# Alternating load queues, a fourth buffer for `a`, a seventh for the output and an earlier load of `a` in a tuned batched 64x64 matmul

## The chip, the cores and the metric

The kernel runs on one core of a Trainium2 chip. The metric is the device time of a run in microseconds, given as the median of a kernel's runs. Times of single events are microseconds from the start of the profiled span.

## The reference

```python
def reference(a, b):                       # a, b: (1024, 64, 64) float32
    return np.matmul(a, b).astype(np.float32)
```

There are 1024 independent products of 64x64 matrices: 16.78 MB of a, 16.78 MB of b and 16.78 MB of output cross the pipe to memory, 50.33 MB in all.

## The kernel before

The work is cut into 16 b tiles of 64 matrices (one output tile each) and 8 a tiles of 128 matrices, so that each a tile serves two b tiles. VectorE regroups an a tile (`regroup`), TensorE transposes it, ScalarE copies the transposes out of PSUM, and VectorE spreads them into block-diagonal operands (`spread`). ScalarE casts the b tile to bf16, TensorE multiplies, and the two halves of an output tile are copied out of PSUM by ScalarE (first half) and VectorE (second half). Three queues carry the transfers: SyncE's and ScalarE's bring b and the first a tile, and GpSimd's brings all other a tiles (casting them from fp32 to bf16 on the way) and takes all stores. The parts that the change and the argument touch:

```python
    A_AHEAD = 3                            # a buffers
    B_AHEAD = 4                            # b buffers
    ...
    o_pool = ...tile_pool(name="o_pool", bufs=6)             # output tiles in SBUF
    o_psum = ...tile_pool(name="o_psum", bufs=2, space=PSUM) # two half tiles of products
    ...
    def load_a(s):                         # 4 DMAs on GpSimd's queue
        a_sb = a_pool.tile([128, 4, 16, 64], bf16, name="a_sb")
        for h in range(4):
            nc.gpsimd.dma_start(out=..., in_=a_v[s, h])
    ...
    def load_b(t):
        b_sb = b_pool.tile([128, 16, 128], fp32, name="b_sb")
        queue = nc.scalar if t in (1, 4, 6, 7) else nc.sync
        queue.dma_start(out=b_sb[:], in_=b_v[t])
    ...
        for half in range(2):              # in multiply(t)
            o_ps = o_psum.tile([128, 4, 2, 2, 64], fp32, name="o_ps")
            ...                            # 32 matmuls
            copy = nc.vector.tensor_copy if half else nc.scalar.copy
            evacuate(o_ps, 4 * half, 4, copy)
    ...
        load_first_a()
        ...
        for t in range(B_AHEAD):
            load_b(t)
        nc.vector.memset(bd_tiles[0][:], 0.0)
        make_identity(nc, identity)
        nc.gpsimd.memset(bd_tiles[1][:], 0.0)
        for s in range(1, A_AHEAD):
            load_a(s)
        regroup(0)
        transpose(0, 0)
        transpose(0, 1)
        spread(0)
        cast(0)
        regroup(1)
        load_a(A_AHEAD)
        transpose(1, 0)
        for t in range(n_t):
            s, half = t // 2, t % 2
            if t + 1 < n_t:
                spread(t + 1)
                cast(t + 1)
            if t + B_AHEAD < n_t:
                load_b(t + B_AHEAD)
            if half == 0:
                if s + 2 < n_s:
                    regroup(s + 2)
                if s + 1 + A_AHEAD < n_s:
                    load_a(s + 1 + A_AHEAD)
            multiply(t)
            ...
            if t >= HOLD - 1:
                store(t - HOLD + 1)        # on GpSimd's queue
```

"b3" below is the b tile with t = 3; "the second a tile" is the one with s = 1, "the seventh" the one with s = 6. In the page's line numbers, L99 is the regrouping, L121 the spread, L165 the copies of the products, L177 the products.

## Time and profile before

The median was 135.51 us. The profiled run was 0.3 us slower than that (135.82) and had this course.

| before | us |
|---|---|
| second a tile landed / its regrouping began | 27.92 / 28.04 |
| seventh a tile's regrouping began, after a wait of 2.56 | 96.58 |
| VectorE's last copy ended | 128.80 |
| last store landed | 132.55 |
| span / outside the span | 134.04 / 1.78 |

Read it as one line: VectorE starts a long run with the second a tile, works nearly without a pause, stops once for the seventh a tile, and 3.75 us after its last copy the last store lands. The prediction shows the profile's lines for it. Two more views are needed later. The first is the page's list of queues (queue, kind, packets, MB, share of the 16 DMA engines' time): q0 is GpSimd's, q1 SyncE's, q10 ScalarE's.

```profile
q0 software_dynamic: 8448, 24.12, 61.7%
q1 hardware_dynamic: 6624, 13.63, 28.7%
q10 hardware_dynamic: 2400, 5.24, 10.3%
q8 instruction: 9, 0.15, 0.4%
```

SyncE carries 12 b tiles and ScalarE 4. Queue 8 moved nine packets of 16 KB, which look like TensorE's own instructions: the kernel has 1,152 matmuls and 1,152 weight loads, and 2,304 is nine times 256 (e14 below, with 256 and 256, has two such packets). The second view is the list of queues between 20 and 27 us alone, while the second a tile is on its way:

```profile
q0 software_dynamic: 491, 0.91, 68.5%
q1 hardware_dynamic: 492, 0.97, 40.6%
```

Two queues are at work, and they get the same number of packets.

### The profile page before, as it was taken

The numbers are of one execution on the slowest core, as the hardware profiler recorded it, in microseconds if no ns is written. First come the engines' busy times: TensorE is split into PE (matmuls) and PEld (weight loads), VectorE is DVE, ScalarE is ACT, GpSimd is POOL, SyncE is SP. The second block draws the span as 40 slices with busy tenths as digits, with TensorE's granted clock in tenths as the row PEclk, the third lists the DMA queues.
The fourth block names the chain that finished last, engine by engine and source line by source line (L and its number), as shares of the span: only waits on it lengthen the run. The fifth ranks groups of instructions, "written<-read, shape, count | busy, mean of one in ns | idle before, by whom it ended". The sixth has DMA issues, their size and how long they took to land.

```text
span 134.0 us, 2820 instructions
## 1 busy us (share of the span) xinstructions
PE 66.2 (49%) x1152; PEld 61.9 (46%) x1152; DVE 105.5 (79%) x145; ACT 86.4 (64%) x125; POOL 43.7 (33%) x55
## 2 busy tenths in 40 slices
PE   0008206903970495849734863696309564466300
PEld 0008106904960485749624752685209463456300
DVE  5720539169899989998999999999299999999940
ACT  3244343991899287959998796679708999363500
POOL 8981215332313240214322244324004031141460
PEclk9999975797799768686998699559955999555555
DMA  3999999999999999999999999999999999999793
GB/s 67 386 360 305 306 284 273 267 301 305 302 280 289 281 396 332 310 289 350 402 359 279 269 367 399 351 270 275 390 397 395 393 397 398 402 406 362 262 313 112
DMA packets 17484, 43.17 MB, mean 322 GB/s; under 512 B 1088, under 2 KB 1088, under 8 KB 17472
## 3 DMA queue, kind: packets, MB, share of 16 engines
q0 software_dynamic: 8448, 24.12, 61.7%
q1 hardware_dynamic: 6624, 13.63, 28.7%
q10 hardware_dynamic: 2400, 5.24, 10.3%
q8 instruction: 9, 0.15, 0.4%
q14 instruction: 3, 0.02, 0.0%
HBM read 33.55 MB, written 16.78 MB: 375 GB/s over the span
## 4 chain that ended last, share of the span: by engine, by line
DMA 62%; DVE 14%; issue 11%; POOL 9%; POOLq 1%; DVEq 0%
DMA a_sb<-in_a_dram 45%; DMA out_dram<-o_sb 17%; DVE o_sb L165 8%; DVE at_bd L121 6%; POOL out_dram L154 3%; POOL a_sb L67 3%; POOL at_bd L205 3%; POOLq L262 1%; POOL identity masks.py:199 0%; DVE a_bf L99 0%; POOL identity masks.py:197 0%; POOLq L154 0%; DVEq L99 0%; POOLq masks.py:199 0%; DVEq L121 0%
## 5 line engine op out<-in xcount | busy, mean ns | idle before, releaser
L177 PEld LDWEIGHTS <-at_bd 128*128 128x128 bf16 x1024 | 43.8, 114 | 45.3 <-DVE o_sb L165 30.4
L177 PE MATMUL o_ps<-b_bf,at_bd 128*128 128x64 bf16 x960 | 43.1, 215 | 40.2 <-DVE o_sb L165 28.5
L121 DVE COPY at_bd<-at_sb 32x1024 f32<-32x1024 f32 x64 | 46.6, 728 | 7.3 <-ACT at_sb L111 5.3
L165 ACT COPY o_sb<-o_ps 64x512 f32<-64x512 f32 x60 | 34.8, 580 | 17.4 <-PE o_ps L177 10.7
L165 DVE COPY o_sb<-o_ps 64x512 f32<-64x512 f32 x60 | 41.3, 689 | 2.2 <-PE o_ps L177 1.3
L154 POOL DMA_DIRECT2D out_dram<-o_sb x20 | 20.9, 1044 | 46.6 <-DVE o_sb L165 22.8
L108 PE MATMUL at_ps<-identity,a_bf 128*128 128x128 f32 x128 | 22.8, 339 | 17.6 <-ACT a_bf L97 10.6
L67 POOL DMA_DIRECT2D a_sb<-in_a_dram x28 | 18.7, 681 | 38.9 <-DMA a_sb<-in_a_dram 28.1
L132 ACT CAST b_bf<-b_sb 128x2048 bf16<-128x2048 f32 x15 | 28.6, 1908 | 3.5 <-DMA b_sb<-in_b_dram 3.5
L108 PEld LDWEIGHTS at_ps<-identity,a_bf 128*128 128x128 f32 x128 | 19.1, 181 | 17.9 <-issue 10.6
L111 ACT COPY at_sb<-at_ps 128x512 f32<-128x512 f32 x32 | 17.8, 588 | 8.3 <-PE at_ps L108 8.1
L99 DVE COPY a_bf<-a_sb 128x4096 bf16<-128x4096 bf16 x7 | 8.6, 1227 | 9.0 <-DMA a_sb<-in_a_dram 8.8
L97 ACT CAST a_bf<-o_sb 128x1024 bf16<-128x1024 f32 x2 | 2.1, 1044 | 4.6 <-DMA o_sb<-in_a_dram 4.6
L165 ACT COPY o_sb<-at_ps 64x256 f32<-64x256 f32 x8 | 2.9, 367 | 3.1 <-PE at_ps L177 3.0
L177 PE MATMUL at_ps<-b_bf,at_bd 128*128 128x64 bf16 x64 | 3.6, 242 | 1.3 <-DVE at_bd L121 1.3
L203 DVE MEMSET at_bd<- 128x4096 f32 x1 | 3.5, 3472 | 0.8 <-issue 0.8
L97 DVE CAST a_bf<-o_sb 128x1024 bf16<-128x1024 f32 x2 | 1.5, 764 | 3.0 <-DMA o_sb<-in_a_dram 3.0
L205 POOL MEMSET at_bd<- 128x4096 f32 x1 | 3.5, 3509 | 0.0
L165 DVE COPY o_sb<-at_ps 64x256 f32<-64x256 f32 x8 | 3.4, 422 | 0.1
L200 ACT ACT_TABLE_LOAD x1 | 1.3, 1283 | 2.3 <-issue 2.3
L139 ACT CAST b_bf<-b_sb 128x512 bf16<-128x512 f32 x2 | 1.1, 614 | 0.4 <-DMA b_sb<-in_b_dram 0.4
L137 DVE CAST b_bf<-b_sb 128x512 bf16<-128x512 f32 x2 | 0.8, 426 | 0.0
(9 smaller groups left out, 1.5 us busy)
## 6 DMA issues: line engine op xcount, KB each, us to landing
out_dram<-o_sb POOLq DMA_DIRECT2D x14, 1024.0 KB, 22.5
a_sb<-in_a_dram POOLq DMA_DIRECT2D x28, 256.0 KB, 19.9
o_sb<-in_a_dram ACTq DMA_DIRECT2D x2, 512.0 KB, 6.9
o_sb<-in_a_dram SPq DMA_DIRECT2D x2, 512.0 KB, 5.9
out_dram<-o_sb POOLq DMA_DIRECT2D x2, 512.0 KB, 6.2
out_dram<-o_sb POOLq DMA_DIRECT2D x4, 256.0 KB, 3.9
b_sb<-in_b_dram SPq DMA_DIRECT2D x12, 0.5 KB, 20.2
b_sb<-in_b_dram ACTq DMA_DIRECT2D x4, 0.5 KB, 16.2
```

What stands on the lines that cost most here:

```text
L67: nc.gpsimd.dma_start(out=a_sb[:, h, :, :].rearrange("p v k -> p (v k)"), in_=a_v[s, h])
L97: copy(a_bf[:, :, h, :], a_sb[h].rearrange("p (v k) -> p v k", v=16))
L99: nc.vector.tensor_copy(a_bf[:], a_sb[:].rearrange("p h v k -> p v h k"))
L108: nc.tensor.transpose(at_ps[:, vo, :], a_cols[:, 4 * vo + 2 * j + wl, :], identity[:])
L111: nc.scalar.copy(at_tiles[s][:, j, :, wl, :, :], at_ps[:].rearrange("p vo (g mp) -> p g mp vo", mp=4),)
L121: nc.vector.tensor_copy(bd[rows, :, :, :, h, :].rearrange("p j g wl mo -> p j (g wl) mo"), at_tiles[t // 2][rows, :, half, :, :, :].rearrange(
L132: nc.scalar.copy(b_bf[:], b_sb[:])
L154: nc.gpsimd.dma_start(out=o_v[t, :, lo : lo + n, :], in_=o_sb[:, lo : lo + n].rearrange("p gh j wl n -> p (gh j wl n)"),)
L165: copy(dst, src)
L177: nc.tensor.matmul(o_ps[:, gl, g % 2, j, :], at_bd[:, j, g, :, u], b_bf[:, g, 64 * u : 64 * u + 64], start=(u == 0), stop=(u == 1),)
L203: nc.vector.memset(bd_tiles[0][:], 0.0)
L205: nc.gpsimd.memset(bd_tiles[1][:], 0.0)
```

## The change

The intent: share the b loads evenly between two queues, bring the second a tile earlier by issuing it after half of GpSimd's memset, and run further ahead with a. The whole diff:

```diff
-    A_AHEAD = 3
+    A_AHEAD = 4
@@
-    o_pool = ctx.enter_context(tc.tile_pool(name="o_pool", bufs=6))
+    o_pool = ctx.enter_context(tc.tile_pool(name="o_pool", bufs=7))
@@ def load_b(t):
-        queue = nc.scalar if t in (1, 4, 6, 7) else nc.sync
+        queue = nc.scalar if t % 2 else nc.sync
@@
-        for t in range(B_AHEAD):
+        for t in range(3):
             load_b(t)
         nc.vector.memset(bd_tiles[0][:], 0.0)
         make_identity(nc, identity)
-        nc.gpsimd.memset(bd_tiles[1][:], 0.0)
-        for s in range(1, A_AHEAD):
+        nc.gpsimd.memset(bd_tiles[1][:, 0], 0.0)
+        load_a(1)
+        nc.gpsimd.memset(bd_tiles[1][:, 1], 0.0)
+        for s in range(2, A_AHEAD):
             load_a(s)
         regroup(0)
         transpose(0, 0)
         transpose(0, 1)
+        load_b(3)
         spread(0)
```

Note the last line: b3 no longer starts with the other first tiles. It is issued by ScalarE, after ScalarE's share of the first transposes.

## The prediction

> **What bounds the kernel now.** I read the page's slices first (forty slices of 3.35 us; digits are tenths busy), to see which resource never rests.
>
> ```profile
> DVE  5720539169899989998999999999299999999940
> ...
> DMA  3999999999999999999999999999999999999793
> GB/s 67 386 360 305 306 284 273 267 301 305 302 280 289 281 396 332 310 289 350 402 359 279 269 367 399 351 270 275 390 397 395 393 397 398 402 406 362 262 313 112
> ...
> HBM read 33.55 MB, written 16.78 MB: 375 GB/s over the span
> ```
>
> The DMA row is 9 from the second slice to the thirty-seventh. The dips in GB/s are no slack: the row counts what is written, and the a tiles are read as fp32 and written as bf16. Summing the trace's packet records by what they read, every stretch of 5 us from 5 to 120 us moves 392 to 412 GB/s, whatever the mix, mean 397. The kernel moves 50.33 MB; at 397 GB/s that is 126.8 us of the 134.0 us span. By 5 us 0.73 MB have moved, 1.85 us' worth, so the start loses 3.15 us. After 120 us 3.82 MB are left, 9.6 us' worth, and they take until the last landing at 132.55: 2.95 us lost, in gaps where the queue waits for results. So if nothing in the transfers gets faster, scheduling can win 2.95 us at most: 135.5 - 2.95 = 132.55 us, 2.2% less.
>
> What decides those 2.95 us is VectorE, whose last copies release the last stores. Its timeline, in parts:
>
> ```profile
> 14.94 2.83 DVE L121 COPY at_bd<-at_sb 32x1024 f32<-32x1024 f32 x4 [5.33 <-ACT at_sb L111]
> ...
> 19.87 1.23 DVE L99 COPY a_bf<-a_sb 128x4096 bf16<-128x4096 bf16 x1 [2.10 <-DMA a_sb<-in_a_dram]
> ...
> 21.02 2.84 DVE L121 COPY at_bd<-at_sb 32x1024 f32<-32x1024 f32 x4
> ```
>
> ```profile
> 28.04 1.23 DVE L99 COPY a_bf<-a_sb 128x4096 bf16<-128x4096 bf16 x1 [4.18 <-DMA a_sb<-in_a_dram]
> ...
> 90.93 3.09 DVE L121 COPY at_bd<-at_sb 32x1024 f32<-32x1024 f32 x4
> 96.58 1.23 DVE L99 COPY a_bf<-a_sb 128x4096 bf16<-128x4096 bf16 x1 [2.56 <-DMA a_sb<-in_a_dram]
> ...
> 125.31 3.49 DVE L165 COPY o_sb<-at_ps 64x256 f32<-64x256 f32 x8
> ```
>
> L99 regroups an a tile (128 matrices, two b tiles). VectorE waits 4.18 us for the second a tile (landed 27.92), runs from 28.04 to 94.02 with pauses under half a microsecond (65.98 us for five a tiles, 13.2 each), waits 2.56 us for the seventh, then runs without a break to 128.8. The chain of waits says the same: the stations before the final run are these loads.
>
> ```profile
> 8.59 19.32 DMA a_sb<-in_a_dram
> ...
> 55.32 21.07 DMA a_sb<-in_a_dram
> ...
> 76.67 19.88 DMA a_sb<-in_a_dram
> ...
> 96.58 0.04 DVE a_bf L99
> ```
>
> So the time is: landing of the second a tile, plus VectorE's work, plus stalls on the way, plus some 5 us of last stores. ScalarE also waits twice for stores that still hold an output buffer (1.75 us before 84.5, 4.32 us before 100.56), beside VectorE's own wait.
>
> **What the Trainium skill says.** "DMA: Bandwidth & Descriptors", section "Issuing engines are not separate DMA queues": all transfers run on the same 16 engines, and several issuers save issue time only. The trace agrees: 403 GB/s with three queues loaded (10 to 15 us), 397 with two (20 to 25 us). The same page, "Queues, rings and completion order": an engine serves the queues in turn, a packet each. That agrees too, and decides the shares: b packets are 2 KB, a packets read 4 KB, and from 10 to 15 us SyncE, ScalarE and GpSimd move 108, 108 and 188 GB/s, near 1:1:2; from 20 to 25 us, with ScalarE's queue empty, 141 and 256. "SBUF — State Buffer", section "SBUF: two separate sides": a two-port VectorE operation locks GpSimd out of writing descriptors. Nothing before 4.7 us tests it here, but it could eat part of the early issue below, since VectorE's memset runs from 1.70 to 5.17.
>
> **Part 1, the split memset.** GpSimd's memset is 3.51 us, and its first a issue starts at 4.71. Half of it (1.75 us) after 1.25 puts the issue at 3.0. The first GpSimd packet followed the issue by 3.9 us (8.61); the same lag gives 6.9. The pipe is full from about 4.5 us, so these 1.7 us are taken from others: at a third of 397 GB/s 0.22 MB, which delays a tile 0 (landed 9.47) by some 0.7 us to 10.2. The first tile on GpSimd (2.10 MB) gets 0.43 MB by 10.2 at 132 GB/s; the other 1.66 MB at 190 take 8.7 us: landing 19.0 instead of 19.75. The second memset half ends near 7.3 and is needed only at about 20: free.
>
> **Part 2, b3 and the odd b tiles on ScalarE's queue.** Before, that queue is empty from 18.66 to 27.6 us, and GpSimd has two thirds of the pipe: its second tile lands at 27.92. After, b3 is issued near 14.4 us, behind b1, and fills just this stretch, so GpSimd stays near 190 GB/s: 2.10 MB / 0.190 = 11.0 us, landing at 19.0 + 11.0 = 30.0. b2 lands near 28.8, so it stays behind this. VectorE's regroup moves from 28.04 to 30.1: 2.1 us worse. Later odd tiles are issued on ScalarE after the cast of b(t+1), not at once after that of b(t), one step of 6.6 us later. Against that they no longer queue behind even tiles: at 108 GB/s a b tile (1.05 MB) takes 9.7 us, and with 3.7 us before the first packet about 13.4 of the 20 us available.
>
> **Part 3, four a buffers, seven output buffers.** In GpSimd's order the stores 0 to 2 move behind one more a tile. Counted in units of 1.05 MB (a tile 2, store 1), the seventh a tile ends at unit 17 instead of 19. Stores are needed one tile later, at units 11, 14, 15, 18, 19, 20 for tiles 7 to 12, where tiles 7 to 12 now need 12, 13, 16, 17, 20, 21. But b tiles run ahead on two queues. My estimate from the rates above: at 92.4 us (33.8 units moved in all) 14.0 b tiles instead of 13.2 have landed, so GpSimd has done 17.2 units, where it did 18.0. Unit 17 comes at about 91.5: the wait of 2.56 us at 96.58 is gone. Unit 18 (store 3) comes near 96.5, and ScalarE's copy of tile 10 waits for it some 3 us, while VectorE reaches its own at 97.4: it is passed on little.
>
> **Sum.** VectorE starts its long run at 30.1 and needs 65.98 us for the same five a tiles: 96.1, where before it resumed at 96.58. The rest is unchanged, so the end moves by -0.5 us: 135.5 - 0.5 = 135.0 us.
>
> **Rivals.** First, the early load comes without the damage: if the second a tile still lands near 28, VectorE keeps its start and loses only the stall of 2.56 us, and the end meets the limit by transfers: 132.6 to 133.0 us. For it: 1.7 us of head start, and one more a tile ahead of the stores. Against it: the queue of b3, by the measured shares. Second, transfers fall behind anyway: store 3 at unit 18 or a3, due at 43.4 us with my landing at 40 to 42.5, stalls VectorE, or ScalarE's later issue starves a cast; one such wait of 2 to 3 us gives 137 to 138. For it: the b queues are now privileged over GpSimd's. Against it: margins of 4 us and more at most other places. Third, descriptors held up by VectorE's memset: the early issue is void, the second tile lands near 30.7, and the time is 135.5 to 136. Two HWDGE queues adding bandwidth, the likely hope behind the change, I discard: the pipe is full with two.
>
> **Range and chances.** The gain (2.56 us) and the loss (2.1 us) are both estimates with an error near 1 us each, so 1.4 together, to which the chance of an added stall is put on the slow side: 133.3 to 136.6. Faster by over 2% means below 132.8, at the edge of what transfers allow: 5%. Slower by over 2%, above 138.2, takes two new stalls: 5%. Within 2%: 90%.
>
> **What would show it.** Right: total still flat near 397 GB/s; first GpSimd packets near 7 us; second a regroup at 29 to 31 us with 6 to 7 us idle before it; no VectorE wait at the seventh; a ScalarE wait on a store near 93 to 97 us. Wrong: the second regroup at 28 or earlier (then the first rival), new VectorE waits between 40 and 94 us (the second), or a flat rate above 405 GB/s, which would undo the limit.

## More of the kernel before

"Outside the span" is the profiled run's time less its span, that is what the program takes beside its first and last recorded instruction.

## The result and the profile after

The changed kernel took 137.14 us (137.12 to 137.74, 4 runs) against 135.51 (135.26 to 135.67, 4 runs). The ratio was 1.0133, with a 95% interval of 1.0101 to 1.0164. Ratios here are the mean time of one kernel's runs over that of the other's of the same rounds, so not quite the ratio of the medians quoted. The change cost 1.3%; the prediction of 135.0 us had the wrong sign, and its range ended at 136.6.

First, the transfers. These are the page's slices of the changed kernel:

```profile
DVE  5720468007999999998899989998999899999940
...
DMA  3999999999999999999999999999999999988693
...
q1 hardware_dynamic: 4512, 9.44, 19.8%
q10 hardware_dynamic: 4512, 9.44, 18.4%
```

The queues are balanced now, and the pipe is exactly as full: summed by what the packets read, 399 GB/s from 5 to 115 us, against 398 before. Balance brought no bandwidth. But VectorE's row has grown a hole at slices eight and nine (00 in place of 16), and it no longer has the dip at slice 29. VectorE's timeline of the changed kernel (start, busy us, engine, line, operation, tiles, shapes, count, idle time before and what ended it) shows both:

```profile
31.49 1.23 DVE L99 COPY a_bf<-a_sb 128x4096 bf16<-128x4096 bf16 x1 [8.22 <-DMA a_sb<-in_a_dram]
...
64.81 2.79 DVE L165 COPY o_sb<-o_ps 64x512 f32<-64x512 f32 x4 [0.77 <-PE o_ps L177]
...
97.89 1.23 DVE L99 COPY a_bf<-a_sb 128x4096 bf16<-128x4096 bf16 x1
```

The wait for the second a tile doubled to 8.22 us. The wait for the seventh is gone: its line has no bracket. In between there are new small waits for TensorE's products, of which the one of 0.77 us is the longest. Step by step:

| us | before | after | difference |
|---|---|---|---|
| regrouping of the second a tile began | 28.04 | 31.49 | +3.45 |
| from there to the seventh, without the stall | 65.98 | 66.40 | +0.42 |
| stall before the seventh | 2.56 | 0 | -2.56 |
| from there to VectorE's end | 32.22 | 32.54 | +0.32 |
| from VectorE's end to the last landing | 3.75 | 3.67 | -0.08 |
| from the last landing to the end of the span | 1.49 | 1.50 | +0.01 |
| outside the span | 1.78 | 2.15 | +0.37 |
| time of the profiled run | 135.82 | 137.74 | +1.92 (sum: +1.93) |

The changed kernel's profiled run was 0.6 us over its median, and that of before 0.3 over its own, so the table explains the profiled pair, 0.3 more than the medians differ by.

The chain of waits moved accordingly. Before, loads of a were the largest part of it, 45% of the span; now only one load is in it, and TensorE's products have come in:

```profile
9.55 21.82 DMA a_sb<-in_a_dram
...
61.23 3.55 PE o_ps L177 x64
```

**Why the second a tile landed at 31.37.** Issuing it early worked. The first two lines are GpSimd's timeline before, the next two the same after:

```profile
1.25 3.51 POOL L205 MEMSET at_bd<- 128x4096 f32 x1
4.71 5.00 POOL L67 DMA_DIRECT2D a_sb<-in_a_dram  x8
```

```profile
1.25 1.80 POOL L205 MEMSET at_bd<- 128x2048 f32 x1
3.00 2.32 POOL L67 DMA_DIRECT2D a_sb<-in_a_dram  x4
```

(Line 67 serves a tiles 1 and 2 before, tile 1 alone after.) The issue moved from 4.71 to 3.00, and GpSimd's first packet from 8.61 to 7.05. What ate it is the next stretch. The list of queues from 20 to 27 us, after:

```profile
q0 software_dynamic: 368, 0.66, 49.5%
q1 hardware_dynamic: 367, 0.75, 30.9%
q10 hardware_dynamic: 369, 0.76, 27.7%
```

Before, two queues took 491 and 492 packets in these 7 us. Now three take 368, 367 and 369: the pipe serves packet by packet in turn, so ScalarE's queue, empty before and now holding b3, cut GpSimd's share from a half to a third. That was predicted, with a landing at 30.0. The rest came afterwards. The same list from 27 to 31.5 us of the changed kernel:

```profile
q0 software_dynamic: 278, 0.51, 59.9%
...
q8 instruction: 1, 0.02, 1.4%
```

One instruction packet of 16 KB ran here, at 28.53 us, for 0.975 us (1.4% of 16 engines' 4.5 us). Before, the first one came at 35.76. The second a tile's last piece is spread over 16 engines; 15 of its 16 shares had landed by 29.88, the last at 31.37. b3's landing shows the same: 15 shares by 29.95, the last at 31.22. One engine had fallen behind, and the whole tile waited for it.

**Why the packet came earlier, and where the new waits come from.** TensorE reached its products in another order. The first line is TensorE's timeline before, the next two after:

```profile
32.17 3.44 PE L177 MATMUL o_ps<-b_bf,at_bd 128*128 128x64 bf16 x64 [5.29 <-issue]
```

```profile
27.32 1.09 PE L177 MATMUL o_ps<-b_bf,at_bd 128*128 128x64 bf16 x32 [1.35 <-ACT o_sb L165]
35.58 1.89 PE L177 MATMUL o_ps<-b_bf,at_bd 128*128 128x64 bf16 x32 [7.17 <-DVE o_sb L165]
```

Before, the first half of the second output tile waits for VectorE's copy of the first tile and starts at 32.17 with the second half right behind it. After, it waits for ScalarE's copy and starts at 27.32. The instructions' waits in the two traces say the same. The diff touches neither PSUM nor TensorE, but the pool that gives out the two PSUM buffers gave them out in the other order. So a part of the change is one that nobody wrote. It goes with the alternation: by the same waits, tile by tile, e1, e2 and e5 below, which alternate, have the order of the changed kernel, and e3, e4, e6, e9, e10, e11 and e13, which do not, that of the kernel before. So what e5, e6 and e13 say of the alternation holds for the two together.

### The profile page after: what moved, and what is told of

Same layout as the page of the kernel before. It is cut to its first block, busy times and chain, and to the rows that moved or that the text cites. A ratio compares the mean times of both kernels' runs of the same rounds, so it can differ in the third digit from the quotient of the medians.

```text
span 135.6 us, 2811 instructions
## 1 busy us (share of the span) xinstructions
PE 66.9 (49%) x1152; PEld 62.7 (46%) x1152; DVE 105.6 (78%) x145; ACT 86.9 (64%) x129; POOL 43.7 (32%) x56
## 4 chain that ended last, share of the span: by engine, by line
DVE 46%; DMA 16%; issue 14%; PE 10%; POOL 9%; POOLq 1%; DVEq 0%
DVE o_sb L165 26%; DVE at_bd L121 19%; DMA a_sb<-in_a_dram 16%; PE o_ps L177 10%; POOL a_sb L67 3%; POOL out_dram L154 3%; POOL at_bd L207 2%; POOL at_bd L205 1%; DVE a_bf L99 1%; POOLq L265 1%; POOL identity masks.py:199 0%; POOL identity masks.py:197 0%; POOLq L154 0%; DVEq L99 0%; POOLq masks.py:199 0%
## 5 line engine op out<-in xcount | busy, mean ns | idle before, releaser
L177 PEld LDWEIGHTS <-at_bd 128*128 128x128 bf16 x1024 | 44.9, 117 | 46.5 <-DVE o_sb L165 41.6
L177 PE MATMUL o_ps<-b_bf,at_bd 128*128 128x64 bf16 x960 | 43.7, 220 | 41.5 <-DVE o_sb L165 38.5
L67 POOL DMA_DIRECT2D a_sb<-in_a_dram x28 | 18.0, 648 | 33.7 <-DMA a_sb<-in_a_dram 29.9
L207 POOL MEMSET at_bd<- 128x2048 f32 x1 | 2.3, 2307 | 0.0
L205 POOL MEMSET at_bd<- 128x2048 f32 x1 | 1.8, 1799 | 0.0
```

The source lines that it names most:

```text
L67: nc.gpsimd.dma_start(out=a_sb[:, h, :, :].rearrange("p v k -> p (v k)"), in_=a_v[s, h])
L177: nc.tensor.matmul(o_ps[:, gl, g % 2, j, :], at_bd[:, j, g, :, u], b_bf[:, g, 64 * u : 64 * u + 64], start=(u == 0), stop=(u == 1),)
L207: nc.gpsimd.memset(bd_tiles[1][:, 1], 0.0)
```

## The experiments

The theory at the start: the late second a tile is the cause, because b3 sits in ScalarE's queue. Rivals: the alternation of the later b tiles holds up GpSimd's queue; the end is bound by the transfers whatever VectorE does; later, the order of the PSUM buffers and the instruction packets. All kernels were correct except the last three, which are wrong. "Base" is the kernel that an edit starts from; ratios are always against the kernel before.

### The start: b3, the memset

**e1_b3_early** (base: after). b3 goes back to the start, on SyncE's queue.

```diff
-        queue = nc.scalar if t % 2 else nc.sync
+        queue = nc.scalar if t % 2 and t != 3 else nc.sync
-        for t in range(3):
+        for t in range(B_AHEAD):
-        load_b(3)
```

> The changed kernel, but b3 is issued at the start on SyncE's queue behind b2, as before. Theory (b3 in ScalarE's queue takes a third of the pipe from the second a tile): ScalarE's queue is empty from about 19 us, the second a tile lands at 27 to 28 us instead of 31.4, VectorE's long run starts 3.5 us earlier and nothing stalls it later, so 133.0 to 133.8 us against 137.1, the limit by transfers being 132.6. Rival (the later stores or the late issue of odd b tiles cost the time): the second a tile may land early, but the end stays at 136.5 to 137.5.

Measured: 136.80 us, ratio 1.0119 (1.0100 to 1.0139). The lines of VectorE's timeline:

```profile
27.33 1.23 DVE L99 COPY a_bf<-a_sb 128x4096 bf16<-128x4096 bf16 x1 [4.03 <-DMA a_sb<-in_a_dram]
...
96.16 2.80 DVE L165 COPY o_sb<-o_ps 64x512 f32<-64x512 f32 x4 [2.02 <-DMA out_dram<-o_sb]
```

The second a tile landed at 27.21, 4.16 us earlier, as the theory had it. The time hardly moved: VectorE gained until it waited for a store (2.02 us), ended at 128.31, and the last store landed 4.8 us after that, at 133.09. So the late tile is not the sole cause (the expectation missed, its rival came true); another limit of like size lies behind it.

**e3_b3_only** (base: before). The late b3 on ScalarE alone.

```diff
-        queue = nc.scalar if t in (1, 4, 6, 7) else nc.sync
+        queue = nc.scalar if t in (1, 3, 4, 6, 7) else nc.sync
-        for t in range(B_AHEAD):
+        for t in range(3):
+        load_b(3)                          # after transpose(0, 1)
```

> The kernel before with one change: b3 late on ScalarE's queue. Theory: the second a tile lands at 30.3 to 31.5 instead of 27.9, but the kernel before waits 2.6 us for its seventh a tile anyway, so most of the delay is absorbed there: 135.5 to 136.5 us. Rival (each us of late start is a us at the end): 138 us or more.

Measured: 135.24 us, ratio 1.0006 (0.9991 to 1.0020).

```profile
30.23 1.23 DVE L99 COPY a_bf<-a_sb 128x4096 bf16<-128x4096 bf16 x1 [5.04 <-DMA a_sb<-in_a_dram]
...
96.17 1.23 DVE L99 COPY a_bf<-a_sb 128x4096 bf16<-128x4096 bf16 x1
```

The tile is 2.2 us later and the stall at the seventh is gone: what VectorE loses at the start, it had been going to lose at the seventh tile anyway. Alone, the late b3 costs nothing. Some 0.7 us of the 2.2 are chance: GpSimd's first packet came at 9.36 here and at 8.61 before. Among the kernels that start as the one before does, it came at 8.6 (before, e4, e11, e12) or at 9.1 to 9.4 (e3, e5, e9, e10, e14, e16), and the second a tile moved with it. So landings of single profiles differ by that much without any cause in the code.

**e2_whole_memset** (base: after). GpSimd's memset in one piece, ahead of all a loads.

```diff
-        nc.gpsimd.memset(bd_tiles[1][:, 0], 0.0)
-        load_a(1)
-        nc.gpsimd.memset(bd_tiles[1][:, 1], 0.0)
-        for s in range(2, A_AHEAD):
+        nc.gpsimd.memset(bd_tiles[1][:], 0.0)
+        for s in range(1, A_AHEAD):
```

> The changed kernel with GpSimd's memset whole again, ahead of all a loads. Theory: the first GpSimd packet comes 1.6 us later (8.6 us), the second a tile at 30.5 to 32, so little moves: 136.3 to 137.8 us. Rival (splitting the memset does harm by itself): 135.5 us or less.

Measured: 137.52 us, ratio 1.0181 (1.0151 to 1.0211); second a tile at 31.23. The interval overlaps the changed kernel's, so the split is worth some tenths of a microsecond at most. Here the instruction packet came only at 31.27, after the landing, so the packet is not the reason for this 31.23; the later issue is the likely one (first packet at 9.25, fifteen of sixteen shares landed by 31.12 and not 29.88).

### The queues of the later b tiles

**e5_alternate_only** (base: before). Only the b tiles from 4 on alternate.

```diff
-        queue = nc.scalar if t in (1, 4, 6, 7) else nc.sync
+        queue = nc.scalar if t == 1 or (t > 3 and t % 2) else nc.sync
```

> The kernel before with only the alternation of queues for b4 and later (b3 stays early on SyncE; three a and six output buffers). Theory A (two b queues take half of the pipe and hold GpSimd's queue back, so a tiles and stores come later): the seventh a tile lands at 98 to 100 us instead of 96.55 and the time is 137 to 138.5 us. Theory B (b3 late is what costs, the alternation is harmless): 135.0 to 136.0 us.

Measured: 139.27 us, ratio 1.0301 (1.0276 to 1.0326), the slowest kernel of all.

```profile
99.45 1.23 DVE L99 COPY a_bf<-a_sb 128x4096 bf16<-128x4096 bf16 x1 [3.64 <-DMA a_sb<-in_a_dram]
```

At 92.4 us 14.10 b tiles had landed, against 13.36 before, and GpSimd's queue had moved 17.75 units of 1.05 MB, against 18.54. The b tiles overtook, and the sixth and seventh a tiles came late (the line is the seventh's; the sixth's wait was 0.95 us). With three queues filled, GpSimd gets every third packet and not every second one. This is the first theory's rival, and it is stronger than expected: +4.1 us (0.0301 of 135.24). The changed order of the PSUM buffers is in these 4.1 us; no run has the alternation alone with the old order. That the b tiles overtake does not hang on it: e7 and e8 below, which alternate with a fixed order, had moved 14.04 and 14.09 b tiles and 17.98 and 17.92 units at 92.4 us.

**e6_after_old_queues** (base: after). The old queues for the later b tiles, b3 late as in the change.

```diff
-        queue = nc.scalar if t % 2 else nc.sync
+        queue = nc.scalar if t in (1, 3, 4, 6, 7) else nc.sync
```

> The changed kernel, b3 late on ScalarE as in it, but b4 and later on the queues of before (4, 6, 7 on ScalarE). Theory A (alternation): 135.2 to 136.0 us. Theory B (b3): the second a tile still lands at 30 us or later, VectorE's run ends late, 136.4 to 137.3 us.

Measured: 136.58 us, ratio 1.0101 (1.0065 to 1.0138). Second a tile at 29.89, VectorE's end at 129.39. In the change itself the alternation, with the PSUM order that goes with it, costs little (0.4 us in the ratio, within the intervals): in the changed kernel only 13.31 b tiles had landed at 92.4 us and GpSimd's queue had moved 18.75 units, much as before. It is not the late start that held the b tiles back, since e7 starts as late and had 14.04; it is the slower course of the work up to there, which e7 changes by the order of the PSUM buffers alone.

**e13_undo_both** (base: after). Queues and b3 as before; the split memset and the buffers stay.

```diff
-        queue = nc.scalar if t % 2 else nc.sync
+        queue = nc.scalar if t in (1, 4, 6, 7) else nc.sync
-        for t in range(3):
+        for t in range(B_AHEAD):
-        load_b(3)
```

> The changed kernel with b3 early and b4 and later on the queues of before; the split memset, four a and seven output buffers stay. Theory (late b3 and alternation each hold the kernel near 136.7, so undoing one shows little): both undone, the second a tile lands at 27.3 us, no VectorE wait of over 1 us comes later, 135.3 to 135.8 us, 1.4 to 1.9 less than the change. Rival (what is left, the buffers and the memset, is the cause): 136.5 us or more.

Measured: 135.31 us, ratio 0.9999 (0.9976 to 1.0022).

```profile
27.85 1.23 DVE L99 COPY a_bf<-a_sb 128x4096 bf16<-128x4096 bf16 x1 [4.29 <-DMA a_sb<-in_a_dram]
...
123.77 3.49 DVE L165 COPY o_sb<-at_ps 64x256 f32<-64x256 f32 x8
```

Undoing b3 gave back 0.0014 of the ratio, undoing the alternation 0.0032, undoing both 0.0134, which is all of it (1.8 us). The parts hide each other: each alone keeps the kernel at about the same time. Since the order of the PSUM buffers goes back with the alternation, there are two clean pairs, both on b3: undoing it gives back 0.0014 with the queues and the order of the change (after and e1), and 0.0102 with those of before (e6 and e13). How the rest divides between the alternation and the order is not shown. There is also a disappointment. VectorE ends at 127.26 here, 1.5 us before the old kernel's 128.80, without any stall, and the time does not fall: the last store lands at 131.69, 4.4 us after VectorE.

### The buffers

**e4_buffers_only** (base: before), **e10_a4_o6** (base: before) and **e11_a3_o7** (base: before): both counts of buffers, the first alone, the second alone.

```diff
-    A_AHEAD = 3
+    A_AHEAD = 4                            # e4 and e10
-    ... name="o_pool", bufs=6))
+    ... name="o_pool", bufs=7))            # e4 and e11
```

> The kernel before with four a buffers and seven output buffers only. Theory: the second a tile lands at 27.9 as before, the stall of 2.56 us at the seventh is gone, VectorE ends 2.5 us earlier: 132.8 to 133.5 us. Rival (deeper buffers only move the backlog, stores come later and stall in their turn): 135 to 136 us.

> The kernel before with four a buffers alone. All kernels with four a and seven output buffers lose 2.14 us between time and span, those with three and six 1.78. If the a buffers do that: 2.14 here. The stall at the seventh a tile goes, but the end hangs on the slowest DMA engine: 135.2 to 135.8 us.

> The kernel before with seven output buffers alone. If these cause the longer time outside the span: 2.14 us here, and 1.78 in e10. The stall at the seventh a tile stays: 135.0 to 135.7 us.

Measured: e4 135.67 us, ratio 1.0036 (1.0021 to 1.0050); e10 137.05 us, 1.0136 (1.0122 to 1.0151); e11 135.58 us, 1.0031 (1.0018 to 1.0043). VectorE's and GpSimd's last work in e4, from their timelines:

```profile
122.69 3.49 DVE L165 COPY o_sb<-at_ps 64x256 f32<-64x256 f32 x8
...
126.47 0.72 POOL L154 DMA_DIRECT2D out_dram<-o_sb  x1 [0.34 <-DVE o_sb L165]
```

Before, GpSimd issued this last store at 129.09, so the store goes out 2.6 us sooner in e4, as expected, and yet it lands at 131.98, 5.8 us after VectorE's end and only 0.6 us before the old one. The rival held: the transfers end there whatever VectorE does. In e10, which missed its expectation, the fourth a buffer puts the stores behind one more a tile, and with six output buffers VectorE has to wait for one:

```profile
91.76 2.80 DVE L165 COPY o_sb<-o_ps 64x512 f32<-64x512 f32 x4 [2.22 <-DMA out_dram<-o_sb]
```

So the seventh output buffer is what makes the fourth a buffer bearable. It has its own price, though: the spans of e11's runs are as long as those of the kernel before in the same session (133.4 to 133.7 against 133.3 to 133.6), and yet it is slower. All kernels with seven output buffers spent 2.13 to 2.23 us outside the span, all with six 1.77 to 1.87. That is +0.37 us. Why, the runs do not show.

### The order of the PSUM buffers

**e7_psum_ordered** (base: after), **e12_before_psum** (base: before) and **e8_psum_swapped** (base: after). Two pools of one buffer each, so that each half of an output tile always has the same one; e8 swaps them from the second tile on.

```diff
-    o_psum = ...tile_pool(name="o_psum", bufs=2, space=PSUM)
+    o_psum = [...tile_pool(name=f"o_psum{i}", bufs=1, space=PSUM) for i in range(2)]
-                o_ps = o_psum.tile(...)
+                o_ps = o_psum[half].tile(...)                    # e7 and e12
+                o_ps = o_psum[(half + (t > 0)) % 2].tile(...)    # e8
```

> The changed kernel with each half of a tile in a PSUM buffer of its own (first halves wait for ScalarE's copy, second ones for VectorE's). The pool gave the buffers of the two kernels in different orders, which the diff does not show. If that order costs time: 136.0 us or less. If not: 136.7 to 137.4, and the first instruction fetch at 28.5 us as in the changed kernel.

> As e7_psum_ordered, but from tile 1 on the two buffers swap, so that tile 1's first half waits for VectorE's copy of tile 0, as in the kernel before. TensorE then stops before tile 1, and its first instruction fetch comes at about 36 us instead of 28.5. Theory (that fetch holds up one of the 16 engines by 1.5 us just when the second a tile lands): the second a tile lands at 29.9 instead of 31.4 us and the time is 1.0 to 1.5 us under e7. Rival (chance): same as e7 within 0.3 us, second a tile at 31 or later.

> The kernel before with each half of a tile in a PSUM buffer of its own, as in e7. VectorE reaches the seventh a tile 1.5 us sooner and waits there that much longer, since the tile's landing is set by the queues; the work behind it is as long: 134.8 to 135.4 us. If the order of PSUM buffers also costs at the end: 134 us or less.

Measured: e7 136.16 us, ratio 1.0072 (1.0049 to 1.0094); e8 136.36 us, 1.0097 (1.0055 to 1.0138); e12 135.89 us, 1.0052 (1.0037 to 1.0066). VectorE's timeline of e7 (lines are shifted by three in this file), then of e8:

```profile
31.46 1.23 DVE L102 COPY a_bf<-a_sb 128x4096 bf16<-128x4096 bf16 x1 [8.26 <-DMA a_sb<-in_a_dram]
...
95.85 1.23 DVE L102 COPY a_bf<-a_sb 128x4096 bf16<-128x4096 bf16 x1
```

```profile
30.39 1.23 DVE L102 COPY a_bf<-a_sb 128x4096 bf16<-128x4096 bf16 x1 [6.88 <-DMA a_sb<-in_a_dram]
...
95.85 1.23 DVE L102 COPY a_bf<-a_sb 128x4096 bf16<-128x4096 bf16 x1
```

With the same late start as the changed kernel (31.46), e7 reaches the seventh a tile at 95.85 and not 97.89, and ends VectorE's work at 128.07 and not 130.43. e8, which fixes the buffers the other way round from the second tile on, ends VectorE's work at 128.05, after a start 1.1 us earlier than the changed kernel's. So what the pool gave out cost VectorE up to 2.4 us against a fixed order. Of these, 0.8 us reached the time in e7 (0.0061 of the ratio, between the two ranges of its expectation), because the transfers then set the end: the last landing, 132.41, is 4.3 us behind VectorE. In the kernel before the fixed order helps nothing: e12 was expected to be no slower and was, by 0.5%; there the stall at the seventh tile takes up what is won (2.83 us in place of 2.56). Why it is slower, and not the same, is not shown.

e8 serves a second purpose: its products fall at other times, and its first large instruction packet comes only at 38.44. Its second a tile lands at 30.27, and that of e15 below, which has an eighth of these products, at 30.26. With the packet in the way, the changed kernel has 31.37 and e7 (packet at 28.97) 31.34, with the same queues at work. e6 (packet at 37.75) has 29.89, but its SyncE queue was less full (150 packets from 27 to 31.5 us, against 261). So the packet costs the second a tile 1.1 us, or 1.5 by the gap between its last two shares. The third a tile confirms it: in the fifteen kernels with all products its last share landed 0.7 to 2.3 us after the fifteenth, in e14, e15 and e16, whose first packet comes after 51 us, 0.04 to 0.09 us. That half of e8's expectation held, if with 30.27 for the 29.9 expected; the time that was to follow did not, because the end is bound by the transfers as in e7.

### Instruction packets, and what binds the end

**e9_sync_nops** (base: before). The suspicion was that instruction packets, of which some run late in the kernel, hold back one DMA engine and so set the end. The test adds 1,664 no-ops to SyncE, to make more packets.

```diff
         queue.dma_start(out=b_sb[:], in_=b_v[t])
+        if queue is nc.sync and t > 3:
+            for _ in range(640 if t == n_t - 1 else 128):
+                nc.sync.nop(nofuse=True)
```

> The kernel before with idle instructions (no-ops, 1,664 in all) on SyncE behind its b issues, where it has nothing to do[...]. Theory (each fetch puts one DMA engine behind, and every transfer waits for its slowest engine): more instruction packets than the 9 + 3 of before, the last of the 16 engines further behind the first, and a longer time, 136 to 138 us. Rival (fetches are harmless): 135.0 to 135.6 us.

Measured: 135.23 us, ratio 0.9998 (0.9981 to 1.0014). The trace records the same nine large and three small instruction packets as before, so the test did not make what it was to test. It is inconclusive.

**e14_buffers_few_mm** (base: e4), **e15_after_few_mm** (base: after), **e16_before_few_mm** (base: before). Most packets are taken away: one product of 256 columns stands for eight of 64. The results are wrong; loads, copies and stores are all there.

```diff
-                for j in range(2):
-                    for u in range(2):
-                        nc.tensor.matmul(
-                            o_ps[:, gl, g % 2, j, :], at_bd[:, j, g, :, u],
-                            b_bf[:, g, 64 * u : 64 * u + 64],
-                            start=(u == 0), stop=(u == 1))
+                if g % 2 == 0:
+                    nc.tensor.matmul(
+                        o_ps[:, gl, :, :, :] as 256 columns, at_bd[:, 0, g, :, 0],
+                        b_bf[:, g : g + 2, :] as 256 columns, start=True, stop=True)
```

> e4_buffers_only with one product in place of eight (wrong results on purpose): every copy, transfer and wait stays, but TensorE runs a quarter of its instructions, so most of the 9 fetches of 16 KB fall away. Theory (the end of e4 hangs on the slowest of 16 DMA engines, put back 1.5 us by a fetch): the last engine is under 1 us behind in the last quarter, last landing near 130.5 instead of 131.98, 134.0 to 135.0 us against 135.67. Rival (something else in the transfers limits): 135.4 us or more.

> The changed kernel with the same cut (wrong results on purpose). Theory: no fetch at 28.5 us, the second a tile lands at 29.7 to 30.2 us instead of 31.4; 135.0 to 136.2 us against 137.1. Rival: second a tile at 31 us or later, 136.8 us or more.

> The kernel before with the same cut (wrong results on purpose). Theory: the seventh a tile lands 1 to 1.5 us earlier, since no engine is behind, and VectorE's end with it: 133.8 to 134.6 us. Rival: 135 us or more.

Measured: e14 135.26 us, ratio 0.9991 (0.9968 to 1.0014); e15 136.24 us, 1.0068 (1.0039 to 1.0097); e16 135.26 us, 0.9993 (0.9964 to 1.0021). In e14 VectorE ends at 125.52, the large instruction packets are down from nine to two, and the last store still lands at 131.69, its slowest engine 1.9 us behind its fastest. So the theory that instruction packets set the end fell. In e15 the second a tile is back at 30.26 (regrouped from 30.38), which agrees with the packet's part in the changed kernel; its time was slightly above the expected range.

What binds the end is visible in all of them without being explained. The last 10 us of e14, as the slices of that window show them (122 to 132 us, 40 slices: busy share of the 16 engines in tenths, and GB/s):

```profile
DMA  9989999999989999999999998999896564210000
GB/s 360 410 328 410 360 377 393 393 360 344 377 311 377 295 344 328 393 328 328 328 295 344 360 311 279 311 377 377 279 344 262 213 262 164 82 49 16 0 0 0
```

GpSimd's queue alone is at work there, with stores always at hand, and the rate sags from near 400 to some 340 GB/s and then fades out over 2 us as the engines finish one after the other. The engines stay busy while the rate sags: each packet takes longer. The median store packet of 4 KB took 165 ns from 115 to 119 us and 190 ns from 126 to 129.5 us; in the kernel before it was 165 and 188, in e16 165 and 188. Nine in ten packets took 179 ns or more in these later windows. So nearly all engines slow down, not one. In e16 the sixteen shares of the last store landed within 0.32 us of each other. Why the packets slow down is open. Over all kernels VectorE's end ranged from 125.5 to 132.6, and no last landing came before 131.69. In some kernels the last landing follows VectorE's end by 3.6 to 3.9 us (before 3.75, after 3.67, e2 3.60, e3 3.57, e5 3.56): the last stores are waited for there. In the others the distance grows, as the transfers have not caught up (e7 4.3, e13 4.4, e1 4.8, e4 5.8, e14 6.2). No version beat the kernel before by more than the noise.

## Why the prediction was wrong, point by point

**The pipe is full, and balance brings nothing:** right. The rate was 399 GB/s against 398.

**The early issue:** right. The first packet was put at 6.9 us and came at 7.05; the first a tile on GpSimd at 19.0, and it came at 19.16. The descriptors were not held up by VectorE's memset: four issues took 2.32 us while it ran. With that the third rival fell; the last list says more on the section that it rests on.

**Second a tile at 30.0 us:** the mechanism was right and the term too small. It landed at 31.37. The shares were as foretold (368, 367 and 369 packets), and without a packet in the way e8 and e15 have 30.27 and 30.26. The missing 1.4 us are one DMA engine that fell behind while an instruction packet of 16 KB ran: a transfer lands when its slowest sixteenth lands, and the working took the mean rate. That it was such a packet is shown as far as two kernels without it there (e8, e15) had the landing at 30.3 and two with the same queues and with it (after, e7) at 31.3, and by the third a tile.

**"The wait of 2.56 us at 96.58 is gone":** right, and for a simpler reason than the working gave. The estimate of GpSimd's order, 14.0 b tiles and 17.2 units at 92.4 us, did not come true in the changed kernel (13.31 and 18.75); it came near in the alternation alone (14.10 and 17.75). (The estimate also had a slip: 33.8 units less 14.0, and less 2 for the first a tile, which is not on GpSimd's queue, leaves 17.8 and not 17.2.) So the ScalarE wait for a store near 93 to 97 us did not come in the changed kernel. It came where TensorE's order was fixed, in e7 (2.32 us before 94.92, with 14.04 b tiles and 17.98 units), and with an early start, in e1 (landed at 96.06; the estimate was 96.5).

**"VectorE starts its long run at 30.1 and needs 65.98 us for the same five a tiles" and "the rest is unchanged":** this step failed. VectorE needed 66.40, and 32.54 in place of 32.22 afterwards, +0.74 in all. Its waits for products (those over 0.15 us) sum to 1.95 us in place of 1.34, which is most of it. And 0.37 us came outside the span. e7, with a fixed order of the PSUM buffers, has none of these waits and needs 64.4 and 32.2. The 0.32 after the seventh tile are the new order's, since e6 and e13, with the old one, have 32.21 and 32.23; the 0.42 before it are not shown to be, since those two need 67.1 there. e11 shows that the seventh output buffer alone costs the 0.37.

**The sum.** Predicted: 30.1 + 65.98 - 96.58 = -0.50. Measured: -0.50, +1.39 for the start (31.49 in place of 30.1), +0.74 for VectorE's work, -0.08 after VectorE's end, +0.37 outside the span, which is +1.92, as much as the profiled runs differ by. So three terms were missed, of which the landing is the largest.

**The limit by transfers, 132.6 us:** wrong, and the error reached into the chances. The floor was worked out from the mean rate of 397 GB/s up to the last byte, which puts the last landing near 129.6. The earliest seen in a profile was 131.69, even with VectorE done at 125.52 (e14). With the kernel before's 3.27 us from last landing to time (135.82 - 132.55) the floor with six output buffers is about 135.0, an estimate. The kernel before stands 0.2 to 0.5 us above it (medians of 135.51 here and 135.22 to 135.28 in the four later sessions; its lowest run was 134.84). There was next to nothing to win by a change that helps VectorE alone. What slows the store packets at the end, from 165 to some 190 ns, is open. Fewer instruction packets did not cure it (e14, e16). "DMA: Bandwidth & Descriptors", section "Latency and other measured facts", of the Trainium skill says that two of the 16 engines, 7 and 15, are usually slower in traces, and offers the fetching of GpSimd-side descriptors as a best guess. That would fit an engine left behind in a tail carried by GpSimd's queue alone, as in e14; it does not explain that the median packet slowed down. The trace's landings do not name their engine, so no run here shows it.

**The rivals.** The first rival had the second a tile landing near 28 and the time at 132.6 to 133.0. e1 and e13 have that landing (27.21 and 27.73) and no stall at the seventh tile, and took 136.80 and 135.31: the limit behind it was too low. The second rival (new stalls, because b is privileged over GpSimd's queue) was right for the parts: e5 alone makes 139.27, and e10 137.05. The measured 137.14 lies in its range of 137 to 138 by luck: VectorE waited for no store and for no later a tile in the whole change, where the parts partly cancel and another sum came out. That the parts hide each other is shown by e1, e6 and e13.

## What to carry to other kernels

When the transfer pipe is full, moving loads to another queue adds no bandwidth but changes who gets it: count how many queues hold packets in each stretch, since the queue that feeds the critical path gets one share among them. Work out a landing from the slowest of the DMA engines and the end of a kernel from the rate that the last stores get, and neither from the mean rate; here the difference was 1.4 us and 2 us, more than the whole gain expected. Two parts of a change can each be free to undo and expensive together, so undo them in pairs. Compare what the pools give out as well as what the diff says, in the experiments too: here the order of two buffers went along with an edit to the queues.

## What the Trainium skill lacked or had wrong

- "DMA: Bandwidth & Descriptors", section "Issuing engines are not separate DMA queues": true that nothing but issue time is saved, but the section lacks what follows from the engines' taking turns, that the choice of queue shifts the shares. With one queue more in use GpSimd's went from 491 of 983 to 368 of 1,104 packets in 7 us, and alternating queues (with the order of PSUM buffers that came along) cost 3.0% in e5.
- "Runtime: NRT & Kernel Launch", section "Instruction fetch mechanics", lacks what its blocks of instructions do to data beside them: nine packets of 16 KB for 2,304 TensorE instructions, about 1 us each on one engine, 1.1 to 1.5 us on the landing of a tile that was in flight.
- "DMA: Bandwidth & Descriptors", section "Latency and other measured facts", has slow engines but not a slowing of nearly all store packets at the end: from a median of 165 ns to 190 ns in e14, so that with VectorE done at 125.52 the last landing was still at 131.69, and the rate sank from near 400 to about 340 GB/s.
- "SBUF — State Buffer", section "SBUF: two separate sides": nothing wrong was found. Beside VectorE's memset, which it excludes on this chip, no lock was seen: four issues by GpSimd took 2.32 us during it, against 5.00 for eight before, of which only the first 0.5 us were beside it. Beside VectorE's copies there is a slowing that fits the lock: in the kernel before, 11 of the 64 spread copies took 0.77 to 1.03 us, each beside a DMA issue by GpSimd, and of the 20 with no issue beside them none took over 0.69; GpSimd's issue of a at 28.20, beside the regrouping, took 1.19 us, and that at 26.23, beside neither, 0.53.
- No page has that one more output buffer costs time outside the span (1.78 to 2.14 us, e11), nor that 1,664 no-ops on SyncE bring no recorded instruction packet (e9).
